# A hybrid attention layer on one core: neighbourhood values stored as whole token rows and gathered by the heads, with loads and row tiles placed anew

## The chip, the cores and the metric

The kernel runs on one core of a Trainium2 chip. The metric is device time of one execution in microseconds (us). A core has five engines with instruction streams of their own: TensorE (PE in the profile, with its weight loads as PEld), VectorE (DVE), ScalarE (ACT), GpSimd (POOL) and SyncE (SP). Here SP only issues DMAs, in the order of its own queue. Engines wait for each other through semaphores. Within a stream the order is fixed when the program is built: an instruction that has to wait holds up everything behind it on the same engine.

## The reference, cut to what matters

One layer of a transformer trunk in float32: 1024 latent tokens on a grid 64 wide (16 rows), 256 context tokens, model width 1024. It is a half-step feed-forward, then two attentions side by side on one normalised input, then a second half-step feed-forward. The change lies in the projections that feed the attentions and in the first of them, the neighbourhood attention (NA):

```python
qa, ka, va, cq, ckv, kr, gates = jnp.split(h @ w_in, IN_SPLITS, axis=-1)
...
def row(r):
    rs = jnp.clip(r - kh // 2, 0, n_rows - kh)
    ...
    k_b = jnp.moveaxis(lax.dynamic_slice_in_dim(kg, rs, kh, axis=1)[:, :, key_col], 2, 1)
    v_b = jnp.moveaxis(lax.dynamic_slice_in_dim(vg, rs, kh, axis=1)[:, :, key_col], 2, 1)
    ...
    s_loc = jnp.einsum('bjqhd,bjakhd->bhjqak', q_r, k_b).astype(jnp.float32) + bias.astype(jnp.float32)
    s_loc = jnp.where(valid[:, :, None, :], s_loc, neg).reshape(B, H, n_blk, NA_QCOLS, n_loc)
    s_ctx = jnp.einsum('bjqhd,bkhd->bhjqk', q_r, k_ctx).astype(jnp.float32)
    p = jax.nn.softmax(jnp.concatenate([s_loc, s_ctx], axis=-1), axis=-1).astype(v.dtype)
```

There are 8 heads of 64 channels. The 64 grid columns are cut into four blocks of 16 query columns; each block reads 32 key columns, starting at column 0, 8, 24 and 32 (`KSTART`), in a window of 8 rows, and all 256 context keys. The second attention (MLA) has 8 heads over all 1280 tokens, with keys and values from a low-rank latent of 256 channels and queries from one of 768.

## The kernel before, in words

**Arithmetic.** A float32 operand is split into a rounded high part and the rest (the low part); a product is two or three TensorE passes that add up in PSUM (`mm3`: high x high, high x low, low x high). Line 154 is any matmul, line 157 any transpose on TensorE. Line 120 is a wrapper through which most VectorE, ScalarE and GpSimd instructions are recorded, line 132 issues every DMA, all from SP.

**Order.** A `Plan` holds a list of main steps (groups of matmuls). `spread(steps, first, last)` hangs side steps (loads, splits, evictions) on numbered main steps, and `store` hands a DMA to SP two main steps later. With these numbers the program's order is written out by hand, and for what goes through the wrappers of lines 112 to 157 it is kept as written. The instructions of an attention item (`NaItem`, `head_out`, called as `nc.vector`, `nc.scalar`, `nc.gpsimd`) are not held: a scheduler sets their place in each engine's stream when the program is built, by its own idea of how long everything takes, loads included. TensorE's stream is always as written.

**Stages around the change**, with the time at which they run in the profiled execution. `TokenQuarters`, 28 steps from `lat_at` (about 1157 us): the latent tokens' values `va`, low-rank latent and rotary key, for eight tiles of 128 tokens; `tokens.done(t)` puts tile t away. `values_out` splits the tile's values into a tile `v` of 128 tokens x (8 heads x (64 high, 64 low)), and stores it. For each of the four column blocks j there is a DRAM array `vws[j]` in the form in which a head wants it (8 heads x 128 x 512), so every tile is written by eight stores of 32 tokens x 8 heads x 128. Next `context_step`, 8 steps from `c_at` (about 1223 us), does the same for the context; its weights `wva` and `wc` come in by `context_load(j)`, two steps' worth at a time, and are split by `context_split`. Next `side_k`, 4 steps (from about 1257 us), makes the context's NA keys; their weights `winT` are loaded by `raw_load(("k", i), ...)` and split by `side_weight`. Then `kv_heads(0)`, `(1)`, `(2)`: keys and values of the MLA heads for tokens 0 to 511, 512 to 1023 and the context; `wuq`, the weight for the MLA queries, is loaded and split beside them (`q_weight`). Then `q_heads(0)` and `(1)` (about 1304 to 1360 us).

**The NA loop** (about 1368 to 1480 us) runs over 32 items, 8 heads by 4 blocks. Item n has three parts: local, context, edge. Each transposes a piece of the softmax weights (TensorE), copies it rounded (ScalarE, line 1848), subtracts that from the original for the low part (VectorE, line 1849), and multiplies it with values (TensorE, `weigh`). Between the parts stand the scores of item n + 3, in two halves: per half four matmuls into PSUM, then on VectorE one instruction that adds the bias and takes the row maximum (line 1815; the orders print it as ISA, the profile as CUSTOM_DVE_ANT_0, each with a short read of the accumulator), a copy with maximum of the context scores (line 1790), a reduce of the maxima (line 1822), then two exponentials on ScalarE (line 1824) and a reciprocal (line 1828). `head_out` puts the head's result away: copies on ScalarE (lines 1762, 1763 and 1766; the first two for every other item), a sum on VectorE (line 1767, called o below), three instructions on GpSimd (lines 1768 to 1771). The loads of a head (`NaHead.loads`) are issued by SP a head ahead: queries and context keys, keys, first bias, values of blocks 0 and 1 (`va`), context values and second bias, values of blocks 2 and 3 (`vb`), third bias. Blocks 1 and 2 use the second bias. Buffers come from pools: "u" and "v" tiles of 128 x 1024, "t" of 128 x 512, "w" of 128 x 1024 for the heads.

Of the kernel before, what the change touches and what calls it, by code (L numbers as in the profile page):

```python
# [12 lines left out]
ALU = mybir.AluOpType  # L13
AX = mybir.AxisListType

P = 128
# [27 lines left out]
def hybrid_block(ctx: ExitStack, tc: tile.TileContext, a: dict, out: bass.AP):  # L44
# [37 lines left out]
    def DR(shape):  # L82
        n = nm("d")
        return dp.tile(shape, F32, tag=n, name=n)
# [1265 lines left out]

    vws = [DR([NH, P, 512]) for _ in range(4)]
    vcs = DR([NH, P, 256])
# [14 lines left out]
    def values_out(t, pieces):  # L1367
        v = U(F32R)
        vv = v.rearrange("p (h c) -> p h c", h=NH)
        for h, src in pieces:  # L1370
            pv = src.rearrange("p (h c) -> p h c", c=64)
            hs = slice(h, h + pv.shape[1])
            split_to(vv[:, hs, 0:64], vv[:, hs, 64:128], pv)
        if t < 8:
            for j in range(4):
                for r in range(2):
                    row = 2 * t + r
                    o, q = 64 * r + KSTART[j], (row % 4) * 32
                    g = (row // 4) * P
                    store(vws[j][:, q:q + 32, g:g + P].rearrange("h p c -> p h c"),  # L1380
                          f32(v[o:o + 32, :]).rearrange("p (h c) -> p h c", h=NH))
        else:
            g = (t - 8) * P
            store(vcs[:, :, g:g + P].rearrange("h p c -> p h c"), f32(v).rearrange("p (h c) -> p h c", h=NH))
# [105 lines left out]
    plan.spread([lambda: context_banks("mm")], lat_at + 16, lat_at + 17)  # L1490
    plan.spread([lambda k=k: hc2_step(k) for k in range(KD)], lat_at + 17, lat_at + 25)
    plan.spread([lambda: context_banks("ss")], c_at, c_at + 1)
    plan.spread([lambda: context_banks("ms")], c_at + 8, c_at + 9)
    for j in range(4):
        plan.spread([lambda j=j: context_load(j)], c_at - 6 + 2 * j, c_at - 5 + 2 * j)
        plan.spread([lambda j=j: tokens.done(j)], lat_at + 20 + j, lat_at + 21 + j)
        plan.spread([lambda j=j: tokens.done(4 + j)], lat_at + 25 + j, lat_at + 26 + j)
    for k in range(KD):
# [42 lines left out]

    plan.spread([rotate_keys], c_at + 4, c_at + 5)

# [37 lines left out]
    class NaHead:  # L1581
# [33 lines left out]
        def values(self, v, j):  # L1615
            o = (j % 2) * 512
            ld(f32(v[:, o:o + 512]), vws[j][self.h])

# [100 lines left out]
    plan.spread([lambda k=k: wukv.append(kv_weight(k)) for k in range(2)], o, o + 2)  # L1719
    plan.spread([scale_latent], o + 1, o + 2)  # L1720
    for ci, x in ((0, 2), (1, 4), (2, 9)):
        plan.spread(calls(latent_cols(ci, 6, 8, ck, "u", ckv[ci]), 2), o + x, o + x + 2)
    plan.spread([scale_latent], o + 8, o + 9)
    plan.spread([lambda i=i: raw_load(("k", i), a["winT"][4 + i], 1024, "v") for i in range(4)], o + 3, o + 7)
    plan.spread([lambda i=i: side_weight(i) for i in range(4)], o + 6, o + 10)
# [4 lines left out]
    plan.spread([lambda d=d: q_cols(0, d) for d in range(6)], o, o + 9)  # L1730
    o = len(plan.main)
    plan.step(*calls(kv_heads(1, ckv[1]), 9))
    plan.spread([lambda k=k: raw_load(("q", k), a["wuq"][k], QR) for k in range(6)], o - 6, o + 6)
    plan.spread([lambda k=k: wuq.append(q_weight(k)) for k in range(6)], o - 3, o + 9)
    o = len(plan.main)
    plan.step(*calls(kv_heads(2, ckv[2]), 7))
    plan.spread([lambda d=d: q_cols(1, d) for d in range(6)], o, o + 12)
    plan.spread([lambda: qrow.append(gate_rows(qstat[1]))], len(plan.main) - 2, len(plan.main) - 1)
# [631 lines left out]
```

## Time and profile before

| | us |
|---|---|
| median of 3 runs | 2572.18 |
| lowest and highest run | 2571.57, 2572.33 |
| the profiled execution, its own time | 2570.67 |
| its span, first to last instruction | 2568.9 |
| TensorE busy in the span | 2524.9 (98%) |
| VectorE, ScalarE, GpSimd busy | 1960.9, 1275.6, 224.0 |
| mean granted TensorE clock | 0.996 of full |

The span leaves out about 1.8 us around the instructions. The busy time of TensorE has modelled ends, so a full PE is not PE at its peak; the granted clock says at what share of its full pace it ran. A row of a timeline gives start, duration, engine, line, operation, output and input names, shapes and the number of instructions it stands for; a bracket at its end gives the idle time of the engine just before it and what ended that.

### The profile page before, as it was taken

The page shows a single profiled execution, that of the slowest core. Times are in us where ns is not written, and L with a number is a line of the kernel's source. Part 1 is how long each engine was busy: PE and PEld are TensorE (multiplying, and loading weights), DVE is VectorE, ACT ScalarE, POOL GpSimd, SP SyncE. Part 2 cuts the span into 40 slices and gives each one's busy share as a digit, 9 for nine tenths or more (in the row PEclk, how much of TensorE's full clock was granted, in tenths as well). Part 3 has the DMA queues.
Part 4 walks back from the last instruction along what each step waited for, and adds up shares of the span by engine and source line. Part 5 has one row for each costly group of instructions (what it writes and reads, how often), then busy time and mean ns, then how long its engine had stood idle before and what let it go on. Part 6 is the DMA issues. An engine that isn't in the chain of part 4 may idle for free.

```text
span 2568.9 us, 38214 instructions
## 1 busy us (share of the span) xinstructions
PE 2524.9 (98%) x13368; PEld 2160.0 (84%) x13368; DVE 1960.9 (76%) x3687; ACT 1275.6 (50%) x2417; POOL 224.0 (9%) x372
## 2 busy tenths in 40 slices
PE   8999999999999999999899999999999999999998
PEld 6888888888998888889789999998888888888887
DVE  4789986887776577876668988887886888667777
ACT  5632223445654753434447987873267322233444
POOL 0000000001000000001103522221011000000003
PEclk9999999999999999999899999999999999999999
DMA  8455543943674566753977742206836445326824
GB/s 306 156 174 197 190 152 120 344 130 131 230 275 143 206 208 215 263 167 94 313 294 273 245 105 64 70 22 226 307 133 223 157 151 173 113 99 218 287 70 164
DMA packets 245761, 475.94 MB, mean 185 GB/s; under 512 B 31488, under 2 KB 73152, under 8 KB 245568
## 3 DMA queue, kind: packets, MB, share of 16 engines
q1 hardware_dynamic: 245568, 473.49, 54.7%
q8 instruction: 106, 1.74, 0.3%
q14 instruction: 87, 0.71, 0.1%
HBM read 348.80 MB, written 124.58 MB: 184 GB/s over the span
## 4 chain that ended last, share of the span: by engine, by line
PE 38%; ACT 5%; DVE 5%; issue 2%; DMA 1%; SPq 0%; POOL 0%; POOLq 0%; DVEq 0%; ACTq 0%
PE bs L154 17%; PE bm L154 11%; PE bv L154 8%; ACT xu L1926 2%; DVE xu L1790 2%; PE bm L157 2%; DVE t L1953 1%; ACT t L1952 1%; DMA t<-in_wada 1%; ACT t L1926 1%; ACT t L1766 0%; DMA xu<-in_wuq 0%; ACT t L120 0%; PE bs L157 0%; DVE xu L120 0%
## 5 line engine op out<-in xcount | busy, mean ns | idle before, releaser
L120 ACT CAST xu<-t 128x512 fp32r<-128x512 f32 (+1 forms) x270 | 161.0, 601 | 493.9 <-DVE t L120 351.4
L154 PE MATMUL bm<-xu,xu 128*128 128x512 f32 (+1 forms) x1500 | 356.6, 391 | 0.0
L154 PE MATMUL bs<-xv,xu 128*128 128x512 f32 (+1 forms) x1452 | 347.6, 388 | 1.5 <-DVE xu L120 0.8
L154 PE MATMUL bv<-xv,xu 128*128 128x512 f32 x1342 | 335.5, 389 | 0.0
L154 PEld LDWEIGHTS bm<-xu,xu 128*128 128x128 f32 x1500 | 278.2, 188 | 56.8 <-ACT t L120 0.4
L154 PEld LDWEIGHTS bs<-xv,xu 128*128 128x128 f32 x1452 | 271.9, 188 | 57.9 <-issue 1.1
L154 PEld LDWEIGHTS bv<-xv,xu 128*128 128x128 f32 x1342 | 251.8, 188 | 52.3
L154 PE MATMUL bs<-xv,xv 128*128 128x512 f32 (+1 forms) x1134 | 274.8, 388 | 0.0
L120 DVE TENSOR_TENSOR xu<-xu,xu 128x512 fp32r<-128x512 f32 (+4 forms) x316 | 209.9, 670 | 64.6 <-ACT xu L120 64.3
L154 PEld LDWEIGHTS bs<-xv,xv 128*128 128x128 f32 x1134 | 211.2, 188 | 40.9
L120 DVE TENSOR_TENSOR t<-t,t 128x512 f32<-128x512 f32 (+2 forms) x278 | 185.4, 674 | 43.8 <-ACT t L120 34.5
L154 PE MATMUL bs<-xu,xu 128*128 128x512 f32 (+1 forms) x900 | 216.2, 389 | 1.1 <-DVE t L120 1.1
L154 PE MATMUL bs<-w,w 96*128 96x512 f32 (+3 forms) x832 | 205.8, 366 | 2.8 <-DMA w<-d 1.5
L120 POOL TENSOR_SCALAR st<-st 128x1 f32<-128x1 f32 (+1 forms) x66 | 35.5, 538 | 1949.0 <-ACT t L120 1652.2
L154 PEld LDWEIGHTS bs<-xu,xu 128*128 128x128 f32 x900 | 167.6, 188 | 37.4 <-DVE t L120 1.6
L120 ACT CAST xv<-t 128x512 fp32r<-128x512 f32 x170 | 105.8, 622 | 168.0 <-PE bm L154 69.6
L120 DVE TENSOR_TENSOR xu<-t,xu 128x512 fp32r<-128x512 f32 (+1 forms) x270 | 179.4, 664 | 10.7 <-ACT xu L120 10.6
L154 PE MATMUL bm<-xv,xv 128*128 128x512 f32 (+1 forms) x690 | 182.7, 388 | 0.0
L120 ACT CAST xu<-xu 128x512 fp32r<-128x512 f32 (+1 forms) x226 | 133.8, 602 | 74.6 <-DMA xu<-in_wo 56.9
L154 PE MATMUL bm<-t,xu 128*128 128x256 f32 (+1 forms) x1252 | 157.9, 287 | 8.5 <-ACT xu L120 8.5
L120 DVE TENSOR_TENSOR xv<-t,xv 128x512 fp32r<-128x512 f32 x170 | 117.1, 689 | 62.7 <-ACT xv L120 62.3
L154 PEld LDWEIGHTS bm<-t,xu 128*128 128x128 f32 x1252 | 154.9, 194 | 9.0 <-ACT xu L120 8.7
(249 smaller groups left out, 4290.1 us busy)
## 6 DMA issues: line engine op xcount, KB each, us to landing
d<-t SPq DMA_DIRECT2D x358, 256.0 KB, 2.4
t<-d SPq DMA_DIRECT2D x274, 256.0 KB, 3.9
xu<-in_f1w SPq DMA_DIRECT2D x59, 512.0 KB, 3.9
xu<-in_f2w SPq DMA_DIRECT2D x58, 512.0 KB, 3.8
t<-in_wada SPq DMA_DIRECT2D x112, 256.0 KB, 5.2
xv<-in_f1w SPq DMA_DIRECT2D x44, 512.0 KB, 6.9
xu<-in_winT SPq DMA_DIRECT2D x34, 512.0 KB, 4.5
w<-d SPq DMA_DIRECT2D x32, 512.0 KB, 6.5
```

What stands on the lines that cost most here:

```text
L120: return lambda *x, **y: pin(f(*x, **y))
L154: return pin(nc.tensor.matmul(o, s, m, start=start, stop=stop, skip_group_check=open_group[0]))
L157: return pin(nc.tensor.transpose(o, x, i))
L1790: nc.vector.tensor_scalar(dst, src, 1.0, FMIN, op0=ALU.mult, op1=ALU.max, accum_out=m)
L1926: nc.scalar.activation(x, x, AF.Exp, bias=n_[:, s:s + 1], accum_out=l[:, i:i + 1])
L1952: nc.scalar.copy(t[0], pb)
L1953: nc.vector.tensor_tensor(t[1], pb, f32(t[0]), op=ALU.subtract)
```

## The change

Five parts:

- The four arrays `vws[j]` become one array of 1024 tokens x 1024. `values_out` stores a token tile whole (128 x 1024, 512 KB), one store for eight (8 x 128 KB).
- The heads' loads gather instead: for each block j, four DMAs of 32 x 4 x 128 (64 KB, in pieces of 512 B) for one DMA of 128 x 512 (256 KB). That is 128 gathers for 32 loads. SP's stream goes from 1515 rows to 1475 (neighbouring alike DMAs are one row).
- In `values_out` the low part of a latent tile is subtracted on GpSimd, not on VectorE: 16 instructions of 128 x 384 and 128 x 128 elements.
- Side steps before and around the context stage get other numbers: the context's token tiles (`hc2_step`), `tokens.done` (every second step in place of every step), `context_load` two steps earlier, `winT` two steps earlier, `rotate_keys`, `scale_latent` and `latent_cols` later.
- `kv_heads(2)` comes ahead of `kv_heads(1)`; the loads and splits of `wuq` and the second half of `q_cols` are spread over other steps.

TensorE's instructions are the same 10,257 rows; their order differs in rows 4617 to 5002 (the end of the tokens' steps to `q_heads`).

```diff
@@ -1348,7 +1348,7 @@
             hsteps.extend(hc2[0].fill(xc2, cols["a1"], mod[3]))
         hsteps[k]()
 
-    vws = [DR([NH, P, 512]) for _ in range(4)]
+    vws = DR([NLAT, D])
     vcs = DR([NH, P, 256])
     ck, scaled = {}, []
 
@@ -1370,15 +1370,10 @@
         for h, src in pieces:
             pv = src.rearrange("p (h c) -> p h c", c=64)
             hs = slice(h, h + pv.shape[1])
-            split_to(vv[:, hs, 0:64], vv[:, hs, 64:128], pv)
+            act.copy(vv[:, hs, 0:64], pv)
+            (pool if t < 8 else vec).tensor_tensor(vv[:, hs, 64:128], pv, f32(vv[:, hs, 0:64]), op=ALU.subtract)
         if t < 8:
-            for j in range(4):
-                for r in range(2):
-                    row = 2 * t + r
-                    o, q = 64 * r + KSTART[j], (row % 4) * 32
-                    g = (row // 4) * P
-                    store(vws[j][:, q:q + 32, g:g + P].rearrange("h p c -> p h c"),
-                          f32(v[o:o + 32, :]).rearrange("p (h c) -> p h c", h=NH))
+            store(vws[t * P:(t + 1) * P, :], f32(v))
         else:
             g = (t - 8) * P
             store(vcs[:, :, g:g + P].rearrange("h p c -> p h c"), f32(v).rearrange("p (h c) -> p h c", h=NH))
@@ -1488,13 +1483,13 @@
         banks[0] = x
 
     plan.spread([lambda: context_banks("mm")], lat_at + 16, lat_at + 17)
-    plan.spread([lambda k=k: hc2_step(k) for k in range(KD)], lat_at + 17, lat_at + 25)
+    plan.spread([lambda k=k: hc2_step(k) for k in range(KD)], lat_at + 16, lat_at + 28)
     plan.spread([lambda: context_banks("ss")], c_at, c_at + 1)
     plan.spread([lambda: context_banks("ms")], c_at + 8, c_at + 9)
     for j in range(4):
-        plan.spread([lambda j=j: context_load(j)], c_at - 6 + 2 * j, c_at - 5 + 2 * j)
-        plan.spread([lambda j=j: tokens.done(j)], lat_at + 20 + j, lat_at + 21 + j)
-        plan.spread([lambda j=j: tokens.done(4 + j)], lat_at + 25 + j, lat_at + 26 + j)
+        plan.spread([lambda j=j: context_load(j)], c_at - 8 + 2 * j, c_at - 7 + 2 * j)
+        for t, x in ((j, 21 + 2 * j), (4 + j, (28, 29, 31, 33)[j])):
+            plan.spread([lambda t=t: tokens.done(t)], lat_at + x, lat_at + x + 1)
     for k in range(KD):
         plan.spread([lambda k=k: context_split(k)], c_at - 3 + k, c_at - 2 + k)
     plan.spread(ada_steps((5, 6)), prest, lat_at - 4)
@@ -1539,7 +1534,7 @@
                 vec.tensor_tensor(t2[:, :, o:o + 8], x[:, :, i:i + 8], ss[:, :, o:o + 8], op=ALU.mult)
         vec.tensor_tensor(x, t1, t2, op=ALU.add)
 
-    plan.spread([rotate_keys], c_at + 4, c_at + 5)
+    plan.spread([rotate_keys], c_at + 6, c_at + 7)
 
     qns = [DR([2, P, NLAT]) for _ in range(4)]
     qrs = [DR([2, P, NLAT]) for _ in range(2)]
@@ -1614,7 +1609,10 @@
 
         def values(self, v, j):
             o = (j % 2) * 512
-            ld(f32(v[:, o:o + 512]), vws[j][self.h])
+            src = vws.rearrange("(g r x) c -> r x g c", g=4, r=4)
+            for r in range(4):
+                ld(f32(v[r * 32:(r + 1) * 32, o:o + 512]).rearrange("x (g c) -> x g c", g=4),
+                   src[r, KSTART[j]:KSTART[j] + 32, :, self.h * P:(self.h + 1) * P])
 
     def na_loads(h):
         heads["na", h] = x = NaHead()
@@ -1717,11 +1715,11 @@
     o = c_at
     plan.spread([lambda k=k: raw_load(("kv", k), a["wukv"][k]) for k in range(2)], o - 4, o - 3)
     plan.spread([lambda k=k: wukv.append(kv_weight(k)) for k in range(2)], o, o + 2)
-    plan.spread([scale_latent], o + 1, o + 2)
-    for ci, x in ((0, 2), (1, 4), (2, 9)):
+    plan.spread([scale_latent], o + 6, o + 7)
+    for ci, x in ((0, 2), (1, 7), (2, 10)):
         plan.spread(calls(latent_cols(ci, 6, 8, ck, "u", ckv[ci]), 2), o + x, o + x + 2)
     plan.spread([scale_latent], o + 8, o + 9)
-    plan.spread([lambda i=i: raw_load(("k", i), a["winT"][4 + i], 1024, "v") for i in range(4)], o + 3, o + 7)
+    plan.spread([lambda i=i: raw_load(("k", i), a["winT"][4 + i], 1024, "v") for i in range(4)], o + 1, o + 5)
     plan.spread([lambda i=i: side_weight(i) for i in range(4)], o + 6, o + 10)
     plan.step(*[lambda i=i: side_k(side_w[i], i) for i in range(4)])
     o = len(plan.main)
@@ -1729,12 +1727,12 @@
     plan.spread([lambda d=d: xq.append(load(cqx[d], key="v")) for d in range(6)], o - 3, o)
     plan.spread([lambda d=d: q_cols(0, d) for d in range(6)], o, o + 9)
     o = len(plan.main)
+    plan.step(*calls(kv_heads(2, ckv[2]), 7))
+    plan.spread([lambda k=k: raw_load(("q", k), a["wuq"][k], QR) for k in range(6)], o - 7, o + 5)
+    plan.spread([lambda k=k: wuq.append(q_weight(k)) for k in range(6)], o - 3, o + 12)
+    o = len(plan.main)
     plan.step(*calls(kv_heads(1, ckv[1]), 9))
-    plan.spread([lambda k=k: raw_load(("q", k), a["wuq"][k], QR) for k in range(6)], o - 6, o + 6)
-    plan.spread([lambda k=k: wuq.append(q_weight(k)) for k in range(6)], o - 3, o + 9)
-    o = len(plan.main)
-    plan.step(*calls(kv_heads(2, ckv[2]), 7))
-    plan.spread([lambda d=d: q_cols(1, d) for d in range(6)], o, o + 12)
+    plan.spread([lambda d=d: q_cols(1, d) for d in range(6)], o + 2, o + 14)
     plan.spread([lambda: qrow.append(gate_rows(qstat[1]))], len(plan.main) - 2, len(plan.main) - 1)
     plan.step(*calls(q_heads(0, cqn[0]), 9))
     o = len(plan.main)
```

SP's stream around the context stage. Names: `xu` and `xv` are tiles of the pools "u" and "v", `d_368` to `d_371` the arrays `vws[j]` before, `d_368` the one array after. Before, the stores of the last three token tiles and the key weights behind them read as follows (each row "x2" is two stores):

```order
L132 DMA xv_11645<-in_wva 128x1024
L132 DMA xv_11647<-in_wc 128x704
L132 DMA d_368<-xu_11574 32x8x128 x2
L132 DMA d_369<-xu_11574 32x8x128 x2
L132 DMA d_370<-xu_11574 32x8x128 x2
L132 DMA d_371<-xu_11574 32x8x128 x2
L132 DMA d_368<-xu_11610 32x8x128 x2
...
L132 DMA d_371<-xu_11657 32x8x128 x2
L132 DMA xv_11775<-in_winT 128x1024
L132 DMA xv_11812<-in_winT 128x1024
```

and after, from the last context weights on:

```order
L132 DMA xv_11511<-in_wva 128x1024
L132 DMA xv_11513<-in_wc 128x704
L132 DMA d_368<-xu_11479 128x1024
L132 DMA xv_11632<-in_winT 128x1024
L132 DMA d_368<-xu_11542 128x1024
L132 DMA xv_11662<-in_winT 128x1024
L132 DMA d_368<-xu_11578 128x1024
L132 DMA xv_11703<-in_winT 128x1024
L132 DMA d_368<-xu_11615 128x1024
L132 DMA xv_11724<-in_winT 128x1024
L132 DMA d_368<-xu_11685 128x1024
L132 DMA d_368<-xu_11746 128x1024
```

The key weights moved from behind all stores to places between the third and the seventh.

VectorE's stream in the NA loop, one item of the loop, at the place where the second item of a head has its scores made. Before (`xu_13829` and `xu_13830` are the two halves of that item's weights, `st_13831` its four maxima, `w_13748` the second bias, `bs` the scores in PSUM, `bm` transposed weights, `bv` the result):

```order
L1849 TENSOR_TENSOR t_13819<-bm_13820,t_13818 128x512
L1815 ISA xu_13829,st_13831<-bs_13834,w_13748 128x384
L1815 ISA st_13831 128x1
L1849 TENSOR_TENSOR t_13845<-bm_13846,t_13844 128x512
L1815 ISA xu_13830,st_13831<-bs_13854,w_13748 128x384
L1815 ISA st_13831 128x1
L1790 TENSOR_SCALAR xu_13829,st_13831<-bs_13828 128x256
L1790 TENSOR_SCALAR xu_13830,st_13831<-bs_13828 128x256
L1767 TENSOR_TENSOR t_13867<-t_13867,bv_13813 64x256
L1822 TENSOR_REDUCE st_13832<-st_13831 128x2
L1849 TENSOR_TENSOR xu_13104<-bm_13873,xu_13104 128x2x128
```

After (the same item's weights are `xu_13818` and `xu_13819`, its maxima `st_13820`, the second bias `w_13731`):

```order
L1847 TENSOR_TENSOR t_13808<-bm_13809,t_13807 128x512
L1788 TENSOR_SCALAR xu_13818,st_13820<-bs_13817 128x256
L1847 TENSOR_TENSOR t_13834<-bm_13835,t_13833 128x512
L1765 TENSOR_TENSOR t_13856<-t_13856,bv_13802 64x256
L1847 TENSOR_TENSOR xu_13057<-bm_13862,xu_13057 128x2x128
L1847 TENSOR_TENSOR t_13874<-bm_13875,t_13873 128x512
L1813 ISA xu_13818,st_13820<-bs_13823,w_13731 128x384
...
L1813 ISA xu_13819,st_13820<-bs_13843,w_13731 128x384
...
L1788 TENSOR_SCALAR xu_13819,st_13820<-bs_13817 128x256
L1826 RECIPROCAL st_13750<-st_13749 128x2
L1820 TENSOR_REDUCE st_13821<-st_13820 128x2
L1813 ISA xu_13884,st_13886<-bs_13890,w_13731 128x384
```

The item's two bias additions, its second maximum and its reduce moved behind the item's edge part and the next item's local part; the next item's additions follow them at once. This is so for the second item of heads 1 to 7.

ScalarE's stream at the same place. Before (`xu_13829` and `xu_13830` as above):

```order
L1848 CAST t_13884<-bm_13886 128x512
L1824 ACTIVATE xu_13829,st_13833<-xu_13829,st_13832 128x640
L1848 CAST t_13911<-bm_13913 128x512
L1824 ACTIVATE xu_13830,st_13833<-xu_13830,st_13832 128x640
L1762 COPY t_13934<-bv_13879 64x256
```

and after:

```order
L1846 CAST t_13873<-bm_13875 128x512
L1822 ACTIVATE xu_13818,st_13822<-xu_13818,st_13821 128x640
L1822 ACTIVATE xu_13819,st_13822<-xu_13819,st_13821 128x640
L1846 CAST t_13900<-bm_13902 128x512
L1846 CAST xu_13060<-bm_13934 128x2x128
```

The second exponential moved ahead of the context part's cast.

## The prediction

> **What bounds the kernel now.** I began with the page's busy times, then took stretches of 20 us (columns: stretch, its length, busy time and count of PE, PEld, DVE, ACT and POOL, granted clock, DMA share, GB/s).
>
> ```profile
> PE 2524.9 (98%) x13368; PEld 2160.0 (84%) x13368; DVE 1960.9 (76%) x3687; ACT 1275.6 (50%) x2417; POOL 224.0 (9%) x372
> ```
>
> ```profile
> 1240.00:1260.00 20.00, 11.50 (x57) 10.12 (x56) 7.88 (x19) 5.95 (x14) 0.55 (x2) 0.76 1.00 303
> ...
> 1400.00:1420.00 20.00, 20.00 (x162) 19.89 (x161) 19.55 (x72) 19.29 (x49) 10.46 (x19) 1.00 0.82 288
> ```
>
> TensorE carries the program, so time can be won only where it stands still or runs at a lower clock, and 1240 to 1260 is such a place: 11.5 of 20 us busy, clock 0.76. The neighbourhood attention (1400 to 1420) is the reverse: TensorE is full and VectorE busy for 19.55 of 20. The change touches both. TensorE's own timeline between the tokens' projection and the first heads shows every pause (in brackets: the idle time before, and who ended it), with three rows at full speed to measure by:
>
> ```profile
> 1213.40 1.54 PE L154 MATMUL bs<-xv,xu 128*128 128x400 f32 x7 [0.79 <-DVE xu L120]
> 1215.33 1.18 PE L154 MATMUL bs<-xv,xu 128*128 128x400 f32 x5 [0.38 <-DVE xv L120]
> ...
> 1229.94 0.94 PE L154 MATMUL bv<-xv,t 128*128 128x512 f32 x3
> 1230.71 0.56 PE L154 MATMUL bm<-xv,t 128*128 128x288 f32 x3
> 1231.11 0.86 PE L154 MATMUL bv<-xv,t 128*128 128x512 f32 x3
> ...
> 1235.54 1.95 PE L154 MATMUL bv<-xv,t 128*128 128x512 f32 x3 [2.72 <-ACT xv L120]
> ...
> 1242.10 0.56 PE L154 MATMUL bm<-xv,t 128*128 128x288 f32 x3
> ...
> 1257.04 8.57 PE L154 MATMUL bm<-t,xu 128*128 128x256 f32 x48 [8.50 <-ACT xu L120]
> 1265.45 0.38 PE L157 MATMUL bm<-ident,t 128*128 128x128 f32 x2
> 1265.59 3.12 PE L154 MATMUL bm<-t,xu 128*128 128x256 f32 x24
> 1268.54 0.38 PE L157 MATMUL bs<-ident,t 128*128 128x128 f32 x2
> ...
> 1300.16 1.64 PE L154 MATMUL bs<-xu,xu 128*128 128x512 f32 x6 [1.14 <-DVE t L120]
> 1302.81 0.65 PE L157 MATMUL bs<-ident,st 128*128 128x128 f32 x4 [0.57 <-DVE t L120]
> ...
> 1367.69 1.18 PE L154 MATMUL bs<-w,w 128*128 128x384 f32 x6 [1.52 <-DMA w<-d]
> ```
>
> ScalarE is named as releaser of the two long ones, but it waited itself, and SyncE's queue (next fence) says for what:
>
> ```profile
> 1234.86 0.62 ACT L120 CAST xv<-xv 128x512 fp32r<-128x512 f32 x1 [7.38 <-DMA xv<-in_wva]
> ...
> 1256.37 1.14 ACT L120 CAST xu<-xv 128x512 fp32r<-128x512 f32 x2 [10.44 <-issue]
> ```
>
> ```profile
> 1208.12 8.42 SPq L132 DMA_DIRECT2D d<-xu  x16
> ...
> 1218.61 11.27 SPq L132 DMA_DIRECT2D d<-xu  x16
> 1229.98 0.42 SPq L132 DMA_DIRECT2D xv<-in_wva  x1
> ...
> 1230.99 5.52 SPq L132 DMA_DIRECT2D d<-xu  x8
> ...
> 1237.60 13.87 SPq L132 DMA_DIRECT2D d<-xu  x24
> 1251.88 1.80 SPq L132 DMA_DIRECT2D xv<-in_winT  x4
> ```
>
> Sixty-four stores of values (16+16+8+24) hold the queue for 39.1 us, 0.53 to 0.70 us each. The context's wva, issued at 1229.98 behind sixteen of them, ends the 2.72 us pause; the key weights winT, issued at 1251.88 behind twenty-four, end the 8.50 us one.
>
> **The change part by part, the gains.** *Values stored whole.* The 64 stores become 8 of 512 KB. At 0.42 us an issue (the wva load above) they hold SP for about 3.4 us instead of 39.1. Together with the loads' earlier places this puts wva and winT on their way well before they are wanted: winT now stands between the third and the seventh store. I count as won the 2.72 and 8.50 us and the two slow stretches behind them. From 1235.54 to 1242.10 six groups took 6.56 us; at the pace of 1229.94 to 1231.11 (1.17 a pair) two pairs are 2.34, a third pair's first group 0.77, and four transposes about 0.36: 3.47, so 3.1 lost. The 48 matmuls from 1257.04 to 1265.45 took 8.41; the 24 from 1265.59 to 1268.54 took 2.95, so 48 are 5.90, and 2.5 were lost.
>
> *Outputs of row tiles spread out, and half a split moved to GpSimd.* 0.79 + 0.38 = 1.17 us of TensorE's pauses in the tokens' last steps came from VectorE, which loses sixteen subtractions there and does the rest at wider spacing: 1.17 won. GpSimd takes them over; nothing in the trace shows it in this form, and the rows are its products and square-root steps:
>
> ```profile
> L1771 POOL TENSOR_TENSOR xo<-t,xo 64x256 fp32r<-64x256 f32 x26 | 19.2, 737 | 1.5
> ...
> 1226.59 3.46 POOL L120 TENSOR_TENSOR st<-st,mhalf 128x1 f32<-128x1 f32 x1
> ```
>
> At 737 ns for 256 columns, 384 + 128 columns are about 1.1 + 0.4 us a tile; eight tiles in some 45 us hide that, since only a store waits for them. The other end is the second row: an instruction over one column took 3.46 us beside a dense VectorE. Then the step behind it, a later tile's normalisation and through it the latent's transposes, is late, and the unit buffers stay held longer. I charge 2 us for this and for other new jams, between 0 and 5.
>
> *Query weights earlier, third key/value chunk moved ahead of the second.* Same matmuls in another order; the wuq loads start a step earlier than before and are spread over more steps: the 1.14 and 0.57 us go, 1.7. *Head 1's keys* go ahead of the last pair of stores (two stores are about 1.0 us): 1.0 of the 1.52. *rotate_keys, scale_latent, latent_cols later*: nothing waits for them before the first key/value chunk (side_k, over 20 us of matmuls, covers them); uncovered it would be one VectorE row, under 1 us.
>
> Gains: 2.72 + 3.1 + 8.50 + 2.5 + 1.17 + 1.7 + 1.0 = 20.7, less 2 of jams: 18.7.
>
> **The loss, in the neighbourhood attention.** *Gathers.* A head's values come in 16 pieces of 64 KB instead of 4 of 256 KB: 12 more issues a head at about 0.4 us, 5 us of SP in a head's 15.75 us. In pieces of 512 B the old stores moved 128 KB in 0.53 us at best, 249 GB/s, so a head's 1 MB takes about 4.2 us where 288 GB/s (the DMA rate of that stretch) gives 3.6. DMA is 0.82 busy there, so about 0.04 more: not full. Loads for the next head are issued over 14 us ahead, so I cost them at nothing in themselves; without that cover a head would start about 5 us late.
>
> *Order.* But VectorE's order, fixed when the program is built, has changed: the bias additions of each later head's second item, whose bias now stands behind eight gathers, are written one item later. The order shown above has them (st_13820) after the next item's local part. VectorE and ScalarE work at these durations (pitch from start to start; bias addition 0.47, two copies with maximum 0.69, subtraction of 512 columns 0.61, of 256 columns 0.33, o 0.33, reduce 0.07, reciprocal 0.09):
>
> ```profile
> 1405.36 0.55 DVE L1815 CUSTOM_DVE_ANT_0 xu<-bs,w 128x384 f32<-128x384 f32 x1
> ...
> 1405.83 0.42 DVE L1790 TENSOR_SCALAR_CACHE_REDUCE xu<-bs 128x256 f32<-128x256 f32 x1
> ...
> 1406.52 0.41 DVE L1767 TENSOR_TENSOR t<-t,bv 64x256 f32<-64x256 f32 x1
> 1406.85 0.14 DVE L1822 TENSOR_REDUCE st<-st 128x2 f32<-128x4 f32 x1
> 1406.92 0.41 DVE L1849 TENSOR_TENSOR xu<-bm,xu 128x256 fp32r<-128x256 f32 x1
> 1407.25 0.15 DVE L1828 RECIPROCAL st<-st 128x2 f32<-128x2 f32 x1
> 1407.32 0.66 DVE L1849 TENSOR_TENSOR t<-bm,t 128x512 fp32r<-128x512 f32 x1
> 1407.91 0.54 DVE L1815 CUSTOM_DVE_ANT_0 xu<-bs,w 128x384 f32<-128x384 f32 x1
> ...
> 1477.49 0.14 DVE L1822 TENSOR_REDUCE st<-st 128x2 f32<-128x4 f32 x1
> ```
>
> ```profile
> 1407.03 0.83 ACT L1824 ACTIVATE xu<-xu,st 128x640 f32<-128x640 f32 x1 [0.21 <-DVE st L1822]
> ...
> 1407.86 0.56 ACT L1848 CAST t<-bm 128x512 fp32r<-128x512 f32 x1
> 1408.32 0.83 ACT L1824 ACTIVATE xu<-xu,st 128x640 f32<-128x640 f32 x1
> ...
> 1409.15 0.36 ACT L1762 COPY t<-bv 64x256 f32<-64x256 f32 x1
> ```
>
> The reduce of one item releases its exponentials. From 1406.85 to 1477.49 there are 18 intervals, 3.92 us each, 15.7 a head. After the change, by hand, from reduce to reduce, with ScalarE's new order (both exponentials, 0.82 each, then the cast, 0.47): first interval, 0.2 + 1.64 + 0.47, then VectorE's 0.61 + 0.33 + 0.33 + 0.61 + 2 x 0.47 + 0.35 + 0.09 + 0.07 = 5.6; second, 2.3 of ScalarE again, then 0.61 + 0.07 = 3.0; third, 0.7 until a narrow cast and three copies of 0.36 behind ScalarE's last cast are done, local cast 0.5, exponentials 1.6, cast 0.5, then 0.61 + 0.47 + 0.35 + 0.33 + 0.07 = 5.1; fourth, 2.3, then 0.61 + 0.47 + 0.35 + 0.33 + 0.07 = 4.1. Sum 17.8, so 2.1 us more for each of seven heads: 14.7. From below: one item's work (2 x 0.47 + 0.35 + 0.07, and an item's share of the wait) of 1.4 us stands in the wrong interval, and VectorE's 3.67 us of work in 3.92 gives back 1.0 a head: 0.4, or 3 in all.
>
> **Sum.** -18.7 + 14.7 = -4.0 us. The profiled execution itself took 2570.7 (its span and 1.8 around it), 1.5 under the median 2572.2; the same change from the median gives 2568.
>
> **Rivals.** *B, the order costs little* (0.24): TensorE and VectorE run far enough apart for the late additions to be absorbed. For it: VectorE's quarter of a microsecond of slack an item; against: TensorE has none. -18.7 + 3 gives 2556.5; if only half of the chain shows, 2561.
>
> *C, the clock falls in the attention too* (0.20). In the late interval TensorE waits about 2.1 us at once. A pause of 1.52 us (1367.69) left it at full pace, the one of 2.72 us was followed by 3.1 us of loss. If 2.1 us is enough, seven heads lose up to 3.1 each, 22: -4 + 22 = +18, 2590. It decides the sign from 1.3 us of loss per head on. [...]
>
> *D, the stalls only move* (0.14): the loads stand earlier in the queue but wait for buffers that the longer-held tiles block, the context's first weights above all. For it: ScalarE's 10.44 us are marked as issue and not as a transfer; against: the queue's own rows show it filled with stores. Half of the gain gone: -9.4 + 14.7 = +5, 2577.5.
>
> *A, as summed* (0.42), own range 2561 to 2577.
>
> **How the numbers follow.** About 0.2%, 5.1 us, is what a measurement of this kernel can tell from no change: faster is below 2567.0, slower above 2577.3. Faster: B's 0.24 and 0.20 of A; same: 0.20 of A and 0.04 of D; slower: C's 0.20, 0.10 of D and 0.02 of A. The likeliest case is A, 2568; the range 2555 to 2589 takes in B's lower bound and most of C.
>
> **What would show it.** Right: no pause over 1 us on TensorE between 1230 and 1305 and a clock of 1.0 there; eight stores with gaps between them on SP; in the attention, reduces at alternating distances near 5.6, 3.0, 5.1, 4.1 with TensorE idle once per head, from head 1 on. Wrong: evenly spaced reduces at 3.9 (B), a granted clock under 0.9 between 1380 and 1500 (C), a wait of ScalarE for in_wva or in_winT (D), or GpSimd rows of several microseconds in front of a store.

## The result, and the profile after

The changed kernel takes 2583.85 us (median of 6 runs, 2582.07 to 2585.55) against 2571.88 for the kernel before beside it: a ratio of 1.005, 95% interval 1.0037 to 1.0063. It is 12 us slower. The forecast was 2568, 4 us faster. The profiled execution has a span of 2583.8 us, 14.9 more than before's.

TensorE's timeline of the changed kernel over the place where before had pauses of 2.72, 8.50, 1.14 and 0.57 us:

```profile
1213.07 3.35 PE L154 MATMUL bs<-xv,xu 128*128 128x400 f32 x17 [0.33 <-DVE xv L120]
1233.41 0.73 PE L154 MATMUL bv<-xv,t 128*128 128x512 f32 x2 [0.20 <-DVE xv L120]
1234.59 0.54 PE L154 MATMUL bm<-xv,t 128*128 128x288 f32 x2 [0.32 <-DVE xv L120]
1237.39 0.54 PE L154 MATMUL bm<-xv,t 128*128 128x288 f32 x2 [0.32 <-DVE xv L120]
1245.77 0.50 PE L154 MATMUL bm<-t,xu 128*128 128x256 f32 x2 [0.85 <-ACT xu L120]
1246.86 5.78 PE L154 MATMUL bm<-t,xu 128*128 128x256 f32 x46 [0.58 <-DVE xu L120]
1284.66 0.65 PE L157 MATMUL bs<-ident,st 128*128 128x128 f32 x4 [0.16 <-DVE xu L120]
```

The long pauses are gone, and so are the slow stretches behind them: 46 of the 48 matmuls of the context's keys now take 5.78 us, where all 48 took 8.57. SyncE's queue shows why: the key weights (in_winT) go out singly between whole stores (d<-xu) of 0.33 us each.

```profile
1223.03 0.33 SPq L132 DMA_DIRECT2D xv<-in_winT  x1
1224.43 0.33 SPq L132 DMA_DIRECT2D d<-xu  x1
1225.60 0.33 SPq L132 DMA_DIRECT2D xv<-in_winT  x1
1228.02 0.33 SPq L132 DMA_DIRECT2D d<-xu  x1
1228.44 0.37 SPq L132 DMA_DIRECT2D xv<-in_winT  x1
```

The other side is the neighbourhood attention. The stretches (columns as in the prediction) of the changed kernel:

```profile
1240.00:1260.00 20.00, 18.57 (x134) 17.28 (x133) 14.45 (x32) 10.82 (x24) 1.66 (x4) 1.00 0.87 281
1400.00:1420.00 20.00, 16.72 (x127) 15.89 (x126) 15.96 (x57) 15.40 (x37) 8.23 (x14) 0.98 0.67 220
```

From 1240 to 1260 TensorE is busy 18.57 us instead of 11.50. From 1400 to 1420 it is busy 16.72 instead of 20.00, and VectorE, ScalarE and GpSimd have fallen with it (19.55 to 15.96, 19.29 to 15.40, 10.46 to 8.23): none is full there any more, they wait for each other. TensorE's own waits say for whom:

```profile
1379.23 1.10 PE L154 MATMUL bs<-w,w 128*128 128x256 f32 x4 [2.25 <-DVE st L1813]
...
1388.40 0.63 PE L154 MATMUL bs<-w,w 128*128 128x384 f32 x2 [0.77 <-DVE st L1813]
...
1393.30 0.63 PE L154 MATMUL bs<-w,w 128*128 128x384 f32 x2 [0.70 <-DVE st L1813]
...
1398.92 1.10 PE L154 MATMUL bs<-w,w 128*128 128x256 f32 x4 [1.87 <-DVE st L1813]
```

Scores wait for a PSUM bank that line 1813, the bias addition, has not emptied: about 2 us once a head (seven times, 1.87 to 2.27), and twice a head 0.4 to 0.9 us more.

Two marks bound the loop in every kernel: the first group of eight score matmuls, and the first scores of the second attention. Before and after:

```profile
1363.91 1.79 PE L154 MATMUL bs<-w,w 128*128 128x256 f32 x8 [0.67 <-DVE st L1815]
...
1476.43 0.96 PE L154 MATMUL bs<-w,w 96*128 96x256 f32 x6
```

```profile
1345.77 1.79 PE L154 MATMUL bs<-w,w 128*128 128x256 f32 x8 [0.66 <-DVE st L1813]
...
1489.90 0.96 PE L154 MATMUL bs<-w,w 96*128 96x256 f32 x6
```

So the change wins 18.1 us ahead of the loop, and the loop goes from 112.5 to 144.1 us, a loss of 31.6. The wait of 1.52 us for head 1's keys that the prediction shows at 1367.69 lies inside this loop, and the changed kernel no longer has it; apart from it the loop loses about 33. The second attention's scores start 13.5 us later, nearly all of the 14.9 of the two spans.

### The profile page after: what moved, and what is told of

Its sections match the earlier page's. It is cut to its first block, busy times and chain, and to the rows that moved or that the text cites. A ratio compares the mean times of both kernels' runs of the same rounds, so it can differ in the third digit from the quotient of the medians.

```text
span 2583.8 us, 38291 instructions
## 1 busy us (share of the span) xinstructions
PE 2532.1 (98%) x13368; PEld 2164.3 (84%) x13368; DVE 1964.8 (76%) x3671; ACT 1276.8 (49%) x2417; POOL 236.0 (9%) x388
## 4 chain that ended last, share of the span: by engine, by line
PE 81%; ACT 7%; DVE 6%; issue 3%; DMA 2%; POOL 1%; SPq 0%; DVEq 0%; POOLq 0%; ACTq 0%
PE bs L154 35%; PE bm L154 25%; PE bv L154 18%; PE bm L157 2%; DVE xu L1788 2%; ACT xu L1924 1%; DVE t L1951 1%; ACT t L1950 1%; ACT xu L1822 1%; ACT t L120 1%; DVE xu L120 1%; DVE xv L120 1%; ACT xu L120 1%; PE bs L157 1%; ACT t L1846 1%
## 5 line engine op out<-in xcount | busy, mean ns | idle before, releaser
L120 DVE TENSOR_TENSOR xu<-xu,xu 128x512 fp32r<-128x512 f32 (+2 forms) x300 | 204.2, 684 | 62.4 <-ACT xu L120 62.3
L154 PE MATMUL bs<-w,w 96*128 96x512 f32 (+3 forms) x832 | 211.9, 372 | 24.2 <-DVE st L1813 23.8
L154 PE MATMUL bs<-xu,xu 128*128 128x512 f32 x900 | 216.0, 388 | 0.0
L154 PEld LDWEIGHTS bs<-w,w 96*128 96x128 f32 (+1 forms) x832 | 126.1, 193 | 37.0 <-DVE st L1813 30.0
```

The source lines that it names most:

```text
L120: return lambda *x, **y: pin(f(*x, **y))
L154: return pin(nc.tensor.matmul(o, s, m, start=start, stop=stop, skip_group_check=open_group[0]))
```

## The experiments

Theory 1: the loop's loss is the order of the instructions, set when the program was built. Rival: the gathers themselves, in small pieces and more of them, land late or crowd the queues. Both fit a slower loop; they part once the order is put back while every load stays. Further runs take the storage and the places of the side steps apart.

All the kernels with their two marks, worked out from TensorE's timeline of each profiled execution ("from" is the first group of eight scores, "loop" the time from there to the second attention's first scores), and the median of the runs:

| kernel | from | loop | median |
|---|---|---|---|
| before | 1363.9 | 112.5 | 2570 to 2572 |
| changed | 1345.8 | 144.1 | 2583.9 |
| both orders held | 1347.6 | 112.7 | 2559.3 |
| ScalarE's order held | 1345.0 | 135.6 | 2574.9 |
| VectorE's order held | 1346.3 | 118.4 | 2558.7 |
| old storage, new places | 1360.5 | 112.1 | 2566.1 |
| new storage, old places | 1347.2 | 141.9 | 2583.4 |
| new storage, old places, VectorE held | 1345.6 | 118.4 | 2560.7 |
| biases ahead of the gathers | 1346.3 | 119.6 | 2566.3 |
| before, both held | 1365.1 | 111.9 | 2573.1 |
| both held, split on VectorE | 1346.9 | 113.4 | 2556.5 |
| VectorE held, split on VectorE | 1342.8 | 118.0 | 2558.7 |
| both held in the first attention alone, split on VectorE | 1344.7 | 116.5 | 2556.3 |

Single runs of one kernel lie up to 5 us from their median, most within 3, so medians closer than about 3 us are not told apart here.

### Both orders held

The attention items' VectorE and ScalarE instructions go through the wrappers that keep them as written; nothing else is edited. `head_out` serves the second attention too, so its outputs are held as well.

```diff
-                nc.vector.tensor_tensor_reduce(out=pr[s][:, :384], in0=loc[:, :384],
+                vec.tensor_tensor_reduce(out=pr[s][:, :384], in0=loc[:, :384],
...
-            nc.scalar.copy(oh, src)
-            nc.vector.tensor_tensor(ol, src, f32(oh), op=ALU.subtract)
+            act.copy(oh, src)
+            vec.tensor_tensor(ol, src, f32(oh), op=ALU.subtract)
```

> The changed kernel, with VectorE's and ScalarE's instructions of the attention items kept in the order in which they are written; loads, gathers and GpSimd's part are as in the changed kernel. VectorE's order in the loop is then again the one of the kernel before, item by item (subtraction, bias addition, subtraction, bias addition, two copies with maximum, reduce, sum, edge), and ScalarE's again cast, exponential, cast, exponential. Theory 1 (the order is the cause of the loss in the neighbourhood attention): reduces 3.9 us apart, 15.7 a head, TensorE without waits for line 1813's bias additions, and about 31 us less than the changed kernel, 2553 (2549 to 2558), which is under the kernel before by the 18 us won ahead of the loop. Rival (the gathers themselves: small pieces, more issues, loads that land late): TensorE or VectorE waits for w<-d, reduces stay near 5 us on average, 2578 to 2586.

Measured: 2559.32 us (2555.66 to 2562.07), a ratio of 0.9955, interval 0.994 to 0.997, to the kernel before. The reduces of this kernel (its instructions carry the wrapper's line 120), the first and the last of 26 intervals:

```profile
1360.43 0.16 DVE L120 TENSOR_REDUCE st<-st 128x2 f32<-128x4 f32 x1
...
1461.10 0.16 DVE L120 TENSOR_REDUCE st<-st 128x2 f32<-128x4 f32 x1
```

100.67 us over 26 is 3.87 us an item, 15.5 a head. One stretch of 100 us in this kernel, and the same in the changed one:

```profile
1360.00:1460.00 100.00, 99.98 (x801) 99.37 (x800) 98.34 (x363) 96.42 (x234) 53.32 (x92) 1.00 0.84 256
```

```profile
1360.00:1460.00 100.00, 83.13 (x617) 78.99 (x617) 78.06 (x277) 74.44 (x178) 41.15 (x70) 0.98 0.71 224
```

With the same gathers TensorE is full again, with more transfers in the stretch (256 GB/s), not fewer. The rival falls: with the order back, the gathers leave the loop 112.7 - 112.5 = 0.2 us longer than before. Against the kernel before with the same order held (111.9, a control below) it is 0.8, and 0.65 of that arises in one place: up to a subtraction 7.66 us behind the mark the two run alike on VectorE (1355.30 and 1372.77), and the next reduce comes 12.79 us behind it in the held changed kernel and 12.14 in the control (1360.43 and 1377.25). In between, TensorE's groups of four matmuls of the held changed kernel took 1.49 us (1354.08) and 1.06 (1355.36); in the changed kernel the same two took 1.49 and 1.05 at a granted clock of 0.72 (1480.64), and 1.10 and 0.64 at 1.00 (1398.92). The loss is the order. The time came out 6 us above the expected 2553 and 1 above its range: against the changed kernel the profiled execution starts the loop 1.9 us later and spends about 1.7 more in the second attention, which leaves about 28 of the 31, and 28.5 is the difference of the two spans.

### One order held at a time

ScalarE's alone (the diff's act lines), then VectorE's alone (its vec lines).

> The changed kernel, with only ScalarE's instructions of the attention items kept as written (cast, exponential, cast, exponential, copies, edge cast); VectorE's second items of the heads are still written an item late. If the late bias additions are nearly all of the loss: 2577 to 2584, with the intervals of the changed kernel. If ScalarE's order is nearly all of it: 2553 to 2558. If both share it, as the measured intervals of 5.9, 4.7, 5.9, 3.3 us suggest (only the third and the first contain a late addition): one long interval per head, 7 x about 2 us above 2553, so 2564 to 2572.

Measured: 2574.89 us (2573.99 to 2577.05), loop 135.6. The time falls between the forecasts, under 2577 to 2584 and above 2564 to 2572: the late additions carry most of the loss, but not nearly all. TensorE still has its seven waits for line 1813, 1.88 to 2.26 us each; the shorter ones behind them are gone.

> The changed kernel with only VectorE's instructions of the attention items kept as written; ScalarE's order is the scheduler's, which then puts both exponentials ahead of the context cast in about half of the items. From the loop's length, first long score group to the first scores of the second attention (before 112.5 us, changed 144.1, both held 112.7, ScalarE held 135.6): if the two orders add up, ScalarE's share is 144.1 - 135.6 = 8.5 in all items, so about 4 here: loop 117, time 2563 (2559 to 2567). If an early second exponential only hurts where a late bias addition stands behind it: loop 113, time 2559. If they do not add and either one out of order costs most of it: loop over 130, time over 2575.

Measured: 2558.66 us (2558.22 to 2559.05), loop 118.4. With VectorE's order right, ScalarE's remaining double exponentials, in about half of the items, leave the loop 118.4 - 112.7 = 5.7 us longer. TensorE waits about 0.4 us once in each of six heads, and at the loop's start for head 1's keys:

```profile
1350.48 1.20 PE L154 MATMUL bs<-w,w 128*128 128x384 f32 x6 [1.82 <-DMA w<-d]
```

With ScalarE's right and VectorE's late additions left, 135.6 - 112.7 = 22.9 us remain. So the late additions are by far the larger part; the double exponentials cost 8.5 us on top of them in all items, and 5.7 without them in half of the items. Whether the two simply add is not shown: no run here has the double exponentials of every item beside VectorE's order as written. The forecast for this kernel lay between its cases: the loop is near the first (117), the time (2563, from 2559) came out 4 us lower, at that of the second (2559). The loop's 5.7 us do not show in the medians either (2558.7 against 2559.3 with both held); in the profiled executions the spans are 2557.3 and 2555.3, since with both held, among other things, the loop starts 1.4 us later and the second attention takes 1.2 us more.

### Storage and places apart

The changed kernel with the old arrays, stores and loads (the diff, and the 64 stores with it); then the kernel before with only the new ones, the same edit the other way. "Places" stands for all the rest of the change: the side steps' places, the split on GpSimd and the order of `kv_heads`.

```diff
-    vws = DR([NLAT, D])
+    vws = [DR([NH, P, 512]) for _ in range(4)]
...
-                ld(f32(v[r * 32:(r + 1) * 32, o:o + 512]).rearrange("x (g c) -> x g c", g=4),
-                   src[r, KSTART[j]:KSTART[j] + 32, :, self.h * P:(self.h + 1) * P])
+            ld(f32(v[:, o:o + 512]), vws[j][self.h])
```

> The changed kernel with the four arrays, the 64 stores and the 256 KB loads of the kernel before; all new places of side steps stay. Theory 1: the scheduler then sees the second bias in time and the loop's order is the one of before, 15.7 us a head. Ahead of the loop: if the 64 stores on SP were what delayed the context's and the key weights, much of the stall stays, since 24 to 32 stores still stand around the loads: about half of the 18 us, 2562 (2557 to 2568). If the new places alone do it: 2553. If the storage alone did it: 2570 to 2574.

Measured: 2566.12 us (2563.32 to 2568.36); ratio 0.9984, interval 0.9974 to 0.9993. The loop is as before. Ahead of it only 1363.9 - 1360.5 = 3.4 us are won, where half of the 18 was expected; the time lies in the range forecast. SyncE's queue of this kernel shows the last sixteen stores now behind the key weights, and in front of the next loads:

```profile
1245.01 10.48 SPq L132 DMA_DIRECT2D d<-xu  x16
1255.59 0.91 SPq L132 DMA_DIRECT2D xv<-d  x2
```

ScalarE waits for loads of this kind, and TensorE behind it:

```profile
1266.91 0.72 ACT L120 ACTIVATE xu<-xv,gqkv 128x512 fp32r<-128x512 f32 x1 [2.64 <-DMA xv<-d]
```

```profile
1269.07 0.98 PE L154 MATMUL bm<-xu,xu 128*128 128x256 f32 x6 [1.81 <-DVE xu L120]
1277.68 2.93 PE L154 MATMUL bs<-xu,xu 128*128 128x512 f32 x6 [4.15 <-DVE xu L120]
```

The pauses of 2.72 and 8.50 us are gone, but new ones, these two and four of 0.65 to 1.77 us up to 1298, stand in their place. Earlier places for some loads moved most of the blockade on to what came next in the queue. Just before the longest pause, 4.15 us, ends, ScalarE had waited 3.50 us ahead of a cast (1275.35); that this wait, too, is for a load is not shown.

> The kernel before with the one array, 8 whole stores and the gathers; VectorE splits as before, and all side steps stand where they stood. Theory 1: the loop's order is the changed kernel's (late second items, both exponentials ahead of the cast), so it loses the same 31 us; ahead of the loop the freed SP lets wva and winT go out in time and most of 15 us is won: 2588 (2581 to 2595). If the places and not the stores win the time ahead of the loop: 2600 to 2605. If the loss in the loop came from the new places and not from the gathers: 2553 to 2560.

Measured: 2583.4 us (2582.17 to 2585.48), in the range of Theory 1. The storage alone wins 1363.9 - 1347.2 = 16.7 of the 18.1 us ahead of the loop, and brings nearly the whole loss in it (loop 141.9). It does two things at once for SP's queue, 8 stores for 64 and 4 MB for 8, since the old blocks overlap and store every token's values twice on average; no run parts the number of stores from their bytes. So the new places hardly matter with the new storage. The same kernel with VectorE's order held as well:

> The kernel before with the one array, whole stores and gathers, VectorE's order of the attention items held; side steps at their old places, splits on VectorE. If storage and gathers alone, once the order is right, carry the gain, and the new places only the 1.4 us that the first group of scores showed (1347.2 against 1345.8 without an order held): 2560 (2557 to 2563). If the new places are worth more when the loop no longer hides it: 2564 to 2568. If they cost time: under 2557.

Measured: 2560.68 us (2558.59 to 2564.73), as forecast, and within scatter of the same kernel with new places (2558.66). Its loop starts at 1345.6, no later than there (1346.3): not even the 1.4 us can be told.

### Biases ahead of the gathers

If the second bias stood behind eight gathers in the scheduler's eyes, loading a head's other two biases ahead of its gathers should free it.

```diff
             self.bias = [U() if h == 1 else W(F32)]
             ld(self.bias[0][:, :768], a["bias"][h, 0])
             yield
+            self.bias.append(W(F32))
+            ld(self.bias[1][:, :768], a["bias"][h, 1])
+            yield
+            self.bias.append(U(F32, "y") if h else W(F32))
+            ld(self.bias[2][:, :768], a["bias"][h, 2])
+            yield
+            ld(f32(kvc[:, 256:512]), vcs[h])
             self.va = va = W()
```

> The changed kernel with a head's second and third bias loaded ahead of its gathers instead of between and behind them; no order is held. In the scheduler's stream no item has its bias additions an item late any more, but the two additions are spread otherwise (addition, subtraction, copy, addition, subtraction, copy) and both exponentials still come ahead of the context cast in every item. If the late additions are the larger part, as 135.6 against 144.1 and 112.7 says: loop about 113 + 8.5 = 121, time 2568 (2563 to 2572). If ScalarE's order alone is harmless without late additions: loop 113 to 115, 2560. If the gathers' place behind more loads makes the values late: waits of TensorE for w<-d, over 2575.

Measured: 2566.29 us (2564.71 to 2570.03), loop 119.6. No item is late any more, and 144.1 - 119.6 = 24.5 us of the loop's loss are gone by the place of two loads alone. The 6.9 that stay are not all ScalarE's order: three of TensorE's waits in the loop, 0.85 to 0.88 us each, are marked as waits for a head's loads (w<-d). And the place has a price behind the loop: the second attention's first scores wait 0.60, 0.19 and 1.90 us for w<-d, four of TensorE's matmuls behind them take 1.05 us (1471.89) where 0.64 is the usual (1474.88), and from its first scores to its last that attention takes 264.0 us (259.6 in the changed kernel). So this kernel is 8 us slower than the one with VectorE's order held, though their loops differ by only 1.2.

### A control, the split, and the best version

As a control, the kernel before with both orders held by the same edit:

> The kernel before with its attention items' instructions kept as written, as a control of the means. Its loop already has this order nearly everywhere: same time, 2570 (2568 to 2573), loop 112 to 113 us. If holding the order is itself worth something, the gain of the changed kernel with orders held is partly not the change's: under 2567.

Measured: 2573.1 us (2571.54 to 2577.23), loop 111.9: holding the order is worth nothing in itself; the time is 3 us longer than the 2570.45 beside it, at the edge of what was expected. The gain of the held changed kernels is the change's.

The low parts back on VectorE, with both orders held, with VectorE's alone, and with both held in the first attention alone:

```diff
-            act.copy(vv[:, hs, 0:64], pv)
-            (pool if t < 8 else vec).tensor_tensor(vv[:, hs, 64:128], pv, f32(vv[:, hs, 0:64]), op=ALU.subtract)
+            split_to(vv[:, hs, 0:64], vv[:, hs, 64:128], pv)
```

> The changed kernel with both orders held, and the latent tiles' low parts subtracted on VectorE as before. If GpSimd's slower subtractions jam the tokens' last steps (the 2 us that the prediction charged): 1 to 2 us less than with both orders held, 2557. If VectorE's relief is what removed the pauses of 0.79 and 0.38 us: up to 2 us more, 2561. If neither matters because the wider spacing does it: within 1 us of 2559.

Measured: 2556.46 us (2554.7 to 2559.42).

> The changed kernel with VectorE's order held and the low parts subtracted on VectorE as before. The same split with both orders held gave 2556.5 against 2559.3. If the split on VectorE is worth its 2 to 3 us on its own: 2556 (2554 to 2558). If that difference was scatter between runs: 2558.7, within 1 us.

Measured: 2558.66 us (2556.58 to 2559.27).

> The changed kernel with both orders held in the neighbourhood attention alone, the second attention's outputs left to the scheduler, and the split on VectorE. With both orders held throughout, the second attention took about 261 us from its first scores to its last, with none held 259.3. If holding its outputs costs that: about 2 us less than with both held and the split on VectorE, 2554.5 (2552 to 2557), the best of all. If not: 2556.5.

Measured: 2556.32 us (2554.63 to 2560.06), ratio 0.9946, interval 0.993 to 0.9963. Against their partners (2559.3 and 2558.7) the splits on VectorE are 2.9 us and nothing: no verdict. In the traces the three pauses from 1233 to 1238 (0.20, 0.32, 0.32) are absent with the split on VectorE, and the old ones of 0.79 and 0.38 do not come back (0.33 is left, as with GpSimd): the wider spacing removed those, not GpSimd. Leaving the second attention to the scheduler did not shorten it (261.5 us from its first to its last scores; 260.9 with all held), so that expectation missed. The loop of this last kernel is 3.1 us longer than with everything held (116.5 against 113.4), with waits of TensorE for VectorE of 0.90 and 1.89 us; where they come from was not followed up. The best version is the change with its order held: 2556 to 2559 us, about 0.5% under the kernel before.

## Why the prediction was wrong, step by step

**The gains were right.** 18.7 us were summed; 1.0 of them, for head 1's keys, lies behind the loop's start, so 17.7 stand against the 18.1 measured there. That the loads stood behind SP's 64 stores is the mechanism, as the two storage runs show. One thing was not seen: the prediction credited stores and earlier places together, but the places alone win 3.4 and the stores alone 16.7. The 2 us charged for new jams have the size of the pauses of 0.16 to 0.85 us in the first fence, 2.8 in all.

**The gathers' own cost, nothing, was right**: 0.2 to 0.8 us of loop with the order held.

**The step that failed is the size of the order's loss**: 14.7 us were summed for seven heads, 31.6 measured, or about 33 apart from the wait for head 1's keys that went away. The place and the kind were right: the late additions, about 2 us of TensorE's idle time once in each of heads 1 to 7. Two parts were too small or missing.

*The chain by hand was too short.* It gave 5.6 + 3.0 + 5.1 + 4.1 = 17.8 us a head. The reduces of one head after the change, at a granted clock of 1.00 from 1393 to 1414:

```profile
1393.84 0.14 DVE L1820 TENSOR_REDUCE st<-st 128x2 f32<-128x4 f32 x1
...
1399.72 0.16 DVE L1820 TENSOR_REDUCE st<-st 128x2 f32<-128x4 f32 x1
...
1402.99 0.14 DVE L1820 TENSOR_REDUCE st<-st 128x2 f32<-128x4 f32 x1
...
1408.40 0.14 DVE L1820 TENSOR_REDUCE st<-st 128x2 f32<-128x4 f32 x1
...
1413.29 0.16 DVE L1820 TENSOR_REDUCE st<-st 128x2 f32<-128x4 f32 x1
```

5.88, 3.27, 5.41 and 4.89: the pattern forecast, each interval 0.3 to 0.8 us longer, 19.45 together (the head before it: 6.04, 3.27, 5.88, 4.66). The chain counted one hand-over an interval, 0.2 us from reduce to exponential, and none from ScalarE's cast to the subtraction that waits for it:

```profile
1386.52 0.56 ACT L1846 CAST t<-bm 128x512 fp32r<-128x512 f32 x1
1386.98 0.38 ACT L1846 CAST xu<-bm 128x256 fp32r<-128x256 f32 x1
```

```profile
1387.18 0.69 DVE L1847 TENSOR_TENSOR t<-bm,t 128x512 fp32r<-128x512 f32 x1 [0.66 <-ACT t L1846]
```

ScalarE goes on to its next instruction 0.46 us after the cast's start, the pitch that the chain used; VectorE starts 0.66 after it. Four times a head these 0.2 us are about half of the 1.65 missing from 19.45. The chain also had VectorE ready when the cast was done. In the fourth interval it is not: its own reciprocal waits for the exponentials, and a bias addition and a maximum stand ahead of the subtraction, which starts 1.08 us after the cast's start, where the chain had 0.47:

```profile
1410.22 0.57 ACT L1846 CAST t<-bm 128x512 fp32r<-128x512 f32 x1
```

```profile
1410.35 0.17 DVE L1826 RECIPROCAL st<-st 128x2 f32<-128x2 f32 x1 [0.82 <-ACT xu L1822]
1410.47 0.56 DVE L1813 CUSTOM_DVE_ANT_0 xu<-bs,w 128x384 f32<-128x384 f32 x1
...
1410.95 0.42 DVE L1788 TENSOR_SCALAR_CACHE_REDUCE xu<-bs 128x256 f32<-128x256 f32 x1
...
1411.30 0.69 DVE L1847 TENSOR_TENSOR t<-bm,t 128x512 fp32r<-128x512 f32 x1
```

From one long wait of TensorE to the next, three of six intervals last 19.6 to 19.7 us: 3.93 more a head than before, and 27.5 for seven, against the 14.7 summed. The forecast's lower bound of 0.4 a head rested on VectorE's slack; the waits within the chain left none to give back.

*Rival C came true in part, and A had put the clock at nothing.* Behind four of the seven long waits (1358.01, 1418.52, 1459.38 and 1480.64) TensorE ran at a lower clock, 0.72 or 0.73 in the six microseconds from 1358, 1418, 1459 and 1480, against 1.00 in those from 1379, 1398 and 1439:

```profile
1418.52 1.28 PE L154 MATMUL bs<-w,w 128*128 128x256 f32 x4 [2.27 <-DVE st L1813]
1419.60 1.05 PE L154 MATMUL bv<-t,w 128*128 128x256 f32 x4
...
1480.64 1.49 PE L154 MATMUL bs<-w,w 128*128 128x256 f32 x4 [1.87 <-DVE st L1813]
```

```profile
1398.00:1404.00 6.00, 5.08 (x38) 4.90 (x39) 4.92 (x22) 3.63 (x10) 1.57 (x4) 1.00 0.44 124
1418.00:1424.00 6.00, 5.48 (x29) 5.30 (x30) 3.87 (x17) 2.64 (x6) 0.93 (x2) 0.72 0.30 88
1480.00:1486.00 6.00, 5.36 (x30) 5.36 (x31) 3.88 (x18) 2.71 (x7) 1.02 (x2) 0.72 0.35 83
```

From the end of the wait to the next transposes of `rope` TensorE needs 2.92 us at full clock (behind 1379.23, 1398.92 and 1439.78) and 4.17, 4.47, 4.48 and 4.28 behind the other four: about 5.7 us in all, where C had put up to 3.1 into every head. 27.5 + 5.7 is 33.2, and without the 1.5 for head 1's keys 31.7: the measured 31.6.

**The range held the time, the side did not.** That the range reached 2584 is owed to C's clock in every head, which is not what happened, so that the time lies inside it is in part luck. A, with 0.42, took a chain of engines at little more than the sum of its pitches. That is near its lower bound, and the forecast put the centre there; the term was the one with the fewest rows behind it and nearly as large as the gain.

## What to carry to other kernels

A load that moves or is cut into more pieces can reorder engines that never touch it, where a scheduler sets their order by its own idea of when data arrive (here the loop went from 112.5 to 144.1 us, and was 112.7 with the order held); compare the orders first, and if they changed, hold the old order or put the load earlier before judging the change itself. Here it was worth more to thin out a queue of many small stores (16.7 us) than to move the loads behind it (3.4 us): moving a few loads ahead handed most of the wait to the next ones. A chain by hand over several engines needs a hand-over for each crossing, here about 0.2 us each, and a look at what stands ahead of the waiting instruction on its own engine.

## What was unexpected of the hardware

The length of a pause did not decide whether TensorE's clock fell. In the changed kernel two waits of 1.87 us had different ends: behind 1398.92 the granted clock stayed at 1.00, behind 1480.64 it was 0.72; so had those of 2.25 (1379.23, 1.00) and 2.27 (1418.52, 0.72). The two groups of four matmuls behind a wait took 1.10 and 0.64 us at 1.00, and 1.21 to 1.49 and 1.05 at 0.72 or 0.73. By that pace the other kernels show the same: in the one with both orders held the two groups took 1.49 and 1.06 behind a wait of 1.80 us (1354.08), in the one with ScalarE's order held 1.25 and 1.06 behind one of 1.97, but 1.10 and 0.63 behind one of 2.26 (1357.59):

```profile
1375.68 1.25 PE L154 MATMUL bs<-w,w 128*128 128x256 f32 x4 [1.97 <-DVE st L1813]
1376.72 1.06 PE L154 MATMUL bv<-t,w 128*128 128x256 f32 x4
```

What decided it no run here shows.
